# The beginning of an encoder block in written order: x loaded first, projection blocks two rows at a time

## The chip, the cores and the metric

The kernel runs on one core of one Trainium2 chip. The metric is device time in microseconds (us) of one execution. A core has engines that each work through a queue of their own: TensorE (PE, matmuls; loads of its stationary operand are shown apart as PEld), VectorE (DVE), ScalarE (ACT), GpSimd (POOL) and SyncE (SP), which here issues most of the transfers. [...]

## The reference

One layer of a streaming encoder block on 512 tokens of 1024 features, in float32. What matters here is its beginning:

```python
c_act = jax.nn.silu(c)
ada = c_act @ w_ada[l] + b_ada[l]
sh1, sc1, g1, sh2, sc2, g2 = jnp.split(ada, 6, axis=-1)
h = modulate(rmsnorm(x, norm1_g[l]), sh1, sc1)
z = h @ w_in[l]
gate_b, gate_c, xa, xr, gr = jnp.split(
    z, [CONV_W, 2 * CONV_W, 3 * CONV_W, 3 * CONV_W + LRU_W], axis=-1)
```

Then follow a gated convolution and a gated recurrence on the parts of `z` (the mixer), an output projection with a residual, a second norm, and a retrieval over 16384 experts: queries, top-16 searches, and two large products with the expert tables.

## The kernel before

Features lie on the 128 partitions, tokens along the free axis, so x is eight "rows" of 128 x 512 (`xs`). float32 products are made of three matmuls each: a weight and an activation are split into a high and a low part, and `mm3` (L87) adds high x high, high x low and low x high for each of the eight rows. A projection block is 128 columns of `w_in`: 24 matmuls of 128x128 on 128x512 into one PSUM tile `ps_z`, of which there are three. `load_w` loads a block (512 KB), `split_w` makes its high part on ACT (L75) and its low part on DVE (L80). There are 20 blocks; their order is `order` (L120).

The beginning does this, in program order:

- L49 to L63: small parameters, the identity matrix, constants. `ii`, the integers from which the identity is made, lies in a pool that is closed at once, and `xs` may use its place.
- L95: x in four transfers.
- L194: `cs`, the silu of c. L228: squares of the eight rows on ACT, added up on DVE (L217); column sums by matmul (L200); the root, `rstd1`; spread over all partitions by eight matmuls (`rows_of`, L225) into `psr`.
- L272: four times a "quarter" (`ada_quarter`): it clears a PSUM tile on DVE (L240), loads four pieces of the adaLN weights and multiplies them with `cs` (L245), copies the result (ACT, L248), transposes it (L251), and makes shift and scale of two rows (L256 to L258). Then these two rows are multiplied with `psr` (L275) and modulated (L266 to L268: DVE, ACT, DVE), which gives the high and low part of `h`. A block of `w_in` is loaded between.
- L283 to L311: some 35 tiny operations on 128x4 values for the recurrence's decay.
- L319: a constant matrix of means; L325: `ada_rest`, a generator whose steps make the later adaLN sums (gates and second norm) in between the projection blocks: on TensorE (L139) and on DVE (L156, L160), both from `cs`. Its first step clears `bdr` and loads the recurrence's weights into it.
- L391: the mixer: five projection blocks in each of four rounds (`zblock`), each used by ACT and DVE as soon as it is there.

The order on each engine is not the written one here: up to the two large products a planner arranges all instructions, by the program's order, by what waits for what, and by costs it assumes. Only from L1124 on does the kernel use `tc.manual_schedule()`, a region in which each engine issues its instructions as they are written. Instructions from outside such a region may still be put in between.

Of the kernel before, what the change touches and what calls it, by code (L numbers as in the profile page):

```python
# [34 lines left out]
def block_kernel(ctx, tc, xT, small, w_ada1, w_ada, b_ada, w_in, w_r, w_i, w_out, w_q, keys, uT, u, v, final_g, out):  # L35
# [15 lines left out]
    boot = ExitStack()  # L51
    ii = boot.enter_context(tc.tile_pool(name="boot", bufs=1)).tile([128, 128], I32, name="ii")
# [100 lines left out]

    def ada_sum(q, every):
        acc = piece(0, q, "wacc", 2)
        nc.vector.tensor_scalar(acc, acc, cs[:, 0:1], None, op0=OP.mult)  # L156
        for k in range(1, KB):
            if k % every == 0:
                yield
            nc.vector.scalar_tensor_tensor(acc, piece(k, q), cs[:, k:k + 1], acc, op0=OP.mult, op1=OP.add)  # L160
        return acc

    def ada_gate1():
        pr = ada_rows()
# [58 lines left out]
    def rows_of(ps, rstd):  # L223
        for t in range(NT):
            nc.tensor.matmul(ps[:, t * 128:(t + 1) * 128], rstd[:, t:t + 1].to_broadcast([128, 128]), ident,  # L225
                             start=True, stop=True)

    for k in range(KB):  # L228
        sq_sum(k, False)
    rstd1 = const.tile([128, NT], F32, name="rstd1")  # L230
    rsqrt_small(rstd1, pst, 1.0 / D, NT)
    psr = psA.tile([128, T], F32, name="ps_rs")
    rows_of(psr, rstd1)
# [4 lines left out]
    def ada_quarter(j):  # L238
        pr = psZ.tile([128, 256], F32, name="ps_g", bufs=2)
        nc.vector.memset(pr, 0.0)  # L240
        for k2 in range(4):
            wt = ada0.tile([128, 2, 2, 256], F32, name="wada0")
            nc.sync.dma_start(wt.rearrange("p a b c -> p (a b c)"), w_ada1[4 * j + k2])
            for b in range(4):
                nc.tensor.matmul(pr[32 * b:32 * b + 1, :], cs[:, 2 * k2 + b // 2:2 * k2 + b // 2 + 1],  # L245
                                 wt[:, b // 2, b % 2, :], start=(k2 == 0), stop=(k2 == 3), skip_group_check=True)
        row = ada0.tile([128, 256], F32, name="row0", bufs=2)
        nc.scalar.activation(row, pr, AF.Copy)  # L248
        pc = psA.tile([128, 2, 128], F32, name="ps_row")
        for i in range(2):  # L250
            nc.tensor.transpose(pc[:, i, :], row[:, i * 128:(i + 1) * 128], ident)  # L251
# [6 lines left out]
        nc.vector.scalar_tensor_tensor(A1[:, ks], adac[:, 8 + 2 * j:10 + 2 * j], 1.0, sm("n1g")[:, ks],  # L258
                                       op0=OP.add, op1=OP.mult)

    A1 = const.tile([128, KB], F32, name="A1")
    h1h, h1l = h2h, h2l

# [8 lines left out]
    for j in range(4):  # L272
        ada_quarter(j)
        for k in (2 * j, 2 * j + 1):
            nc.vector.tensor_mul(xn1[:, k, :], xs[:, k, :], psr)  # L275
# [7 lines left out]
    sp = const.tile([128, 4], F32, name="sp")  # L283
    l4 = const.tile([128, 8, 4], F32, name="l4")
    lam = sm("lam")
    z_, tn, e_, w_, w2, ac = (l4[:, i, :] for i in range(6))
    nc.vector.tensor_scalar(z_, lam, -1.0, None, op0=OP.mult)
    nc.vector.tensor_tensor(z_, z_, lam, op=OP.max)
    nc.scalar.activation(tn, z_, AF.Tanh, scale=1.0 / 16)
    nc.vector.tensor_scalar(e_, tn, 1.0, None, op0=OP.add)  # L290
    nc.vector.reciprocal(e_, e_)
    nc.vector.tensor_scalar(tn, tn, -1.0, 1.0, op0=OP.mult, op1=OP.add)
    nc.vector.tensor_mul(e_, e_, tn)
    for _ in range(3):
        nc.vector.tensor_mul(e_, e_, e_)
    nc.vector.tensor_scalar(w_, e_, 2.0, None, op0=OP.add)
    nc.vector.reciprocal(w_, w_)
    nc.vector.tensor_mul(w_, w_, e_)
    nc.vector.tensor_mul(w2, w_, w_)
    nc.vector.memset(ac, 1.0 / 15)  # L300
    for n in range(6, -1, -1):
        nc.vector.tensor_mul(ac, ac, w2)
        nc.vector.tensor_scalar(ac, ac, 1.0 / (2 * n + 1), None, op0=OP.add)
    nc.vector.tensor_mul(ac, ac, w_)
    nc.vector.tensor_scalar(z_, lam, -1.0, 0.0, op0=OP.mult, op1=OP.max)
    nc.vector.tensor_scalar(ac, ac, 8.0, None, op0=OP.mult)
    nc.vector.scalar_tensor_tensor(sp, z_, 4.0, ac, op0=OP.mult, op1=OP.add)
    rg = const.tile([128, 4, 4], F32, name="rg")
    sph, spn, brh, bih = (rg[:, i, :] for i in range(4))
    for dst, src, f in ((sph, sp, 0.5), (spn, sp, -1.0), (brh, sm("br"), 0.5), (bih, sm("bi"), 0.5)):  # L310
        nc.vector.tensor_scalar(dst, src, f, None, op0=OP.mult)  # L311
# [7 lines left out]
    hmean = pers2.tile([128, 128], FR, name="sqa")  # L319
    nc.vector.memset(hmean.bitcast(F32), 0.0)  # L320
    for s in range(2):
        nc.vector.tensor_scalar(hmean[64 * s:64 * s + 64, 64 * s:64 * s + 64], iota[64 * s:64 * s + 64, 0:64],
                                0.0, 1.0 / 64, op0=OP.mult, op1=OP.add)
# [1047 lines left out]
```

## Time and profile before

| | |
|---|---|
| median of 3 runs | 1340.93 us (1340.7 to 1341.18) |
| profiled execution | 1340.21 us |
| its span | 1338.4 us |
| first transfer of x issued | 7.41 us |
| first projection matmul (L89) | 26.87 us |
| first output block evicted (L396) | 46.80 us |
| output projection begins on PE | 164.10 us |

The span is what the profile covers of the execution: from the first to the last instruction. A line of the timeline gives start, duration, engine, line, operation, what it writes and reads, shapes, a count, and in brackets how long its engine had been idle before and whom it waited for. A line of a view by stretches gives the stretch, its length, then busy time and number of instructions of each engine, then TensorE's granted clock (1.00 is full), the share of time in which the DMA engines worked, and GB/s. A step of the chain of waits gives start, duration and what.

### The profile page before, as it was taken

How to read it: one execution, taken by the hardware profiler on the slowest of the kernel's cores; microseconds unless marked ns; L12 is line 12 of the kernel's file. 1: busy time of each engine (PE TensorE's matmuls, PEld its weight loads, DVE VectorE, ACT ScalarE, POOL GpSimd, SP SyncE). 2: the span in 40 equal slices, each digit the busy share in tenths (PEclk: the TensorE clock that was granted, in tenths of full speed). 3: DMA queues.
4: the chain of work that ended last, by engine and by line, in shares of the span. 5: the costliest groups of instructions: out<-in, count | busy, mean ns of one | idle time of the engine just before them, and what ended most of it. 6: DMA issues, size and time to landing. Idle time of an engine off the chain costs nothing.

```text
span 1338.4 us, 21113 instructions
## 1 busy us (share of the span) xinstructions
PE 1300.5 (97%) x7408; PEld 1116.9 (83%) x7408; DVE 1218.1 (91%) x2259; ACT 728.1 (54%) x1319; POOL 506.5 (38%) x336
## 2 busy tenths in 40 slices
PE   5999998999899999999999999999999999999996
PEld 2678776777899999999999998888888888888885
DVE  6899876889999999999989869899989899999898
ACT  4667735423576988878759743333433434333333
POOL 0000000000234113455555627577656565645640
PEclk9999998999999999999999999999999999999999
DMA  9684544242798989999999999999999999999993
GB/s 363 230 297 157 170 146 87 72 167 97 271 352 303 337 314 355 400 396 404 417 395 417 416 370 392 374 396 415 414 414 413 415 413 416 412 410 411 415 373 137
DMA packets 150266, 440.03 MB, mean 329 GB/s; under 512 B 16016, under 2 KB 43664, under 8 KB 150160
## 3 DMA queue, kind: packets, MB, share of 16 engines
q1 hardware_dynamic: 103008, 267.23, 53.6%
q0 software_dynamic: 46864, 170.41, 32.5%
q8 instruction: 58, 0.95, 0.3%
q10 hardware_dynamic: 288, 1.05, 0.2%
q14 instruction: 48, 0.39, 0.1%
HBM read 393.54 MB, written 45.09 MB: 328 GB/s over the span
## 4 chain that ended last, share of the span: by engine, by line
PE 65%; DVE 20%; DMA 6%; issue 5%; ACT 3%; POOL 1%; SPq 0%; DVEq 0%; ACTq 0%; POOLq 0%
PE acc L1196 33%; PE ps_z L89 5%; PE ps_z L90 4%; DVE wlo L80 4%; PE ps_z L91 4%; PE ps_act L89 4%; PE ps_act L91 4%; PE ps_act L90 4%; DVE scr L917 3%; DVE oh L728 2%; DMA wraw<-in_uT_dram 2%; PE ps_gt L761 1%; DMA raw<-in_v_dram 1%; DVE rep L543 1%; ACT igh L749 1%
## 5 line engine op out<-in xcount | busy, mean ns | idle before, releaser
L75 ACT ACTIVATE whi<-wraw 128x1024 fp32r<-128x1024 f32 x255 | 269.9, 1059 | 244.1 <-DMA wraw<-in_v_dram 102.0
L80 DVE TENSOR_TENSOR wlo<-wraw,whi 128x1024 fp32r<-128x1024 f32 x255 | 311.0, 1220 | 45.1 <-ACT whi L75 44.5
L89 PE MATMUL ps_act<-h,whi 128*128 128x320 f32 x928 | 291.4, 314 | 0.0
L91 PE MATMUL ps_act<-h,wlo 128*128 128x320 f32 x928 | 287.0, 309 | 0.9 <-issue 0.9
L90 PE MATMUL ps_act<-h,whi 128*128 128x320 f32 x928 | 286.8, 309 | 0.0
L896 POOL DMA_INDIRECT rows<-in_u_dram,idx_s x128 | 207.5, 1621 | 140.3 <-DVE scr L917 111.7
L896 POOL DMA_INDIRECT rows<-in_v_dram,idx_s x128 | 200.7, 1568 | 152.2 <-DVE ys L934 132.0
L1196 PE MATMUL acc<-whi,cl 128*128 128x512 f32 x744 | 229.1, 389 | 0.1
L1196 PE MATMUL acc<-wlo,ch 128*128 128x512 f32 x744 | 229.1, 389 | 0.0
L1196 PE MATMUL acc<-whi,ch 128*128 128x512 f32 x744 | 229.1, 389 | 0.0
L896 POOL DMA_INDIRECT rows<-in_u_dram,idx_b x64 | 92.0, 1438 | 220.3 <-DVE scr L917 157.5
L91 PEld LDWEIGHTS ps_act<-h,wlo 128*128 128x128 f32 x928 | 174.2, 188 | 1.3 <-issue 1.1
L89 PEld LDWEIGHTS ps_act<-h,whi 128*128 128x128 f32 x928 | 174.2, 188 | 1.1
L90 PEld LDWEIGHTS ps_act<-h,whi 128*128 128x128 f32 x928 | 174.4, 188 | 0.2
L934 DVE SCALAR_TENSOR_TENSOR ys<-rows,acts,ys 128x1024 f32<-128x1024 f32 x127 | 163.3, 1286 | 1.4
L1196 PEld LDWEIGHTS acc<-whi,cl 128*128 128x128 f32 x744 | 139.6, 188 | 29.5 <-DVE cl L1087 0.5
L1196 PEld LDWEIGHTS acc<-wlo,ch 128*128 128x128 f32 x744 | 139.7, 188 | 29.1
L1196 PEld LDWEIGHTS acc<-whi,ch 128*128 128x128 f32 x744 | 139.5, 188 | 28.5
L917 DVE SCALAR_TENSOR_TENSOR scr<-rows,h2n 128x1024 f16<-128x1024 f32 x128 | 156.3, 1221 | 5.9 <-DMA rows<-in_u_dram,idx_s 4.3
L1001 ACT ACTIVATE act<-ps_act 128x320 f32<-128x320 f32 x127 | 56.0, 441 | 101.9 <-PE ps_act L91 64.7
L749 ACT ACTIVATE igh<-oh,gl 128x128 f16<-128x128 f16 x320 | 99.6, 434 | 4.1 <-DVE oh L728 4.1
L488 POOL DMA_DIRECT2D x1d<-xn x8 | 4.6, 570 | 252.2 <-ACT xn L487 251.7
(309 smaller groups left out, 1926.6 us busy)
## 6 DMA issues: line engine op xcount, KB each, us to landing
wraw<-in_uT_dram SPq DMA_DIRECT2D x120, 512.0 KB
wraw<-in_v_dram SPq DMA_DIRECT2D x103, 512.0 KB
Gd<-stg SPq DMA_DIRECT2D x46, 512.0 KB
wada<-in_w_ada_dram SPq DMA_DIRECT2D x45, 512.0 KB
Ad<-act SPq DMA_DIRECT2D x48, 320.0 KB
act<-Ad SPq DMA_DIRECT2D x48, 320.0 KB
raw<-in_v_dram SPq DMA_DIRECT2D x25, 512.0 KB
h<-Gd SPq DMA_DIRECT2D x12, 1024.0 KB
```

The lines of the kernel that those rows point to most:

```text
L75: nc.scalar.activation(hi, raw, AF.Copy)
L80: nc.vector.tensor_sub(lo, raw, hi.bitcast(F32))
L89: nc.tensor.matmul(ps, hi[:, k, :], xh(k), start=first and k == ks[0], stop=False)
L90: nc.tensor.matmul(ps, hi[:, k, :], xl(k), start=False, stop=False)
L91: nc.tensor.matmul(ps, lo[:, k, :], xh(k), start=False, stop=last and k == ks[-1])
L728: nc.vector.tensor_tensor(flat.rearrange("p (q n b) -> p q n b", q=8, b=2), io2[:, None, :, :].to_broadcast(shp), sij[:, a0].rearrange("p ...
L749: nc.scalar.activation(ig[:, 1, k // 2, :, k % 2], of[:, k // 2, 0, :, k % 2], AF.Copy, scale=gl[:, t0 + k:t0 + k + 1])
L896: nc.gpsimd.indirect_dma_start(out=r[:, :], out_offset=None, in_=table, in_offset=bass.IndirectOffsetOnAxis(ap=idxs[:, k:k + 1], axis=0))
L917: nc.vector.scalar_tensor_tensor(scr, rows.pop(n), 1.0, hn, op0=OP.mult, op1=OP.mult, accum_out=dst[:, k:k + 1])
L934: nc.vector.scalar_tensor_tensor(ys, rows.pop(k), acts[:, k:k + 1], ys, op0=OP.mult, op1=OP.add)
L1001: nc.scalar.activation(act[c // 2][:, c % 2], ps, AF.Gelu)
L1196: nc.tensor.matmul(accs[b][e], st[:, bs], mv[:, e * 512:(e + 1) * 512], start=first, stop=last)
```

## The change

The whole beginning, from the first load to the first three projection blocks, is put into a `manual_schedule` region, and is written out in an order by hand.

- `ii` takes a place in the ring of low weight parts; x is loaded right behind the small parameters.
- The decay operations become a generator, `decay`, of which a few are made at a time.
- 30 matmuls of the identity with itself are written ahead of the column sums.
- The root is made by `Abs_reciprocal_sqrt` and four DVE operations instead of `Sqrt`, a reciprocal and five more.
- All loads of blocks and quarters are issued in turn (`quarter_load`); `ada_quarter` is cut into `quarter_mm` (one piece) and `quarter_cols`; `zrows(i, j)` does the six matmuls of block i on the rows 2j and 2j+1. For the first three blocks these are put between the quarters' steps; `zblock` then only hands them out.
- Later adaLN sums read `cl`, a copy of `cs` that is written near the region's end.
- The clearing of `bdr` and the matrix of means move into the region.

```diff
+    begin = ExitStack()
+    begin.enter_context(tc.manual_schedule())
...
-            nc.vector.scalar_tensor_tensor(acc, piece(k, q), cs[:, k:k + 1], acc, op0=OP.mult, op1=OP.add)
+            nc.vector.scalar_tensor_tensor(acc, piece(k, q), cl[:, k:k + 1], acc, op0=OP.mult, op1=OP.add)
...
+    decay_it = decay()
+    next(decay_it)
+    warm = psZ.tile([128, T], F32, name="ps_z", bufs=3)
+    for i in range(NW):
+        nc.tensor.matmul(warm[:, i % 4 * 128:(i % 4 + 1) * 128], ident, ident, start=True, stop=True)
     for k in range(KB):
         sq_sum(k, False)
+        next(decay_it, None)
...
+    def quarter_load(j):
         for k2 in range(4):
...
+    def quarter_mm(j, k2):
+        if k2 == 0:
+            pieces[j] = psZ.tile([128, 256], F32, name="ps_g", bufs=2)
+            nc.vector.memset(pieces[j], 0.0)
+        pr, wt = pieces[j], pieces.pop((j, k2))
+        for b in range(4):
+            nc.tensor.matmul(pr[32 * b:32 * b + 1, :], cs[:, 2 * k2 + b // 2:2 * k2 + b // 2 + 1],
+                             wt[:, b // 2, b % 2, :], start=(k2 == 0), stop=(k2 == 3), skip_group_check=True)
+        if k2 == 3:
+            row = ada0.tile([128, 256], F32, name="row0", bufs=2)
+            nc.scalar.activation(row, pr, AF.Copy)
+            pieces[j] = row
...
+    def zrows(i, j):
+        n = order[i]
+        if n not in zps:
+            zps[n] = psZ.tile([128, T], F32, name="ps_z", bufs=3)
+        for k in (2 * j, 2 * j + 1):
+            mm3(zps[n], *zsp[n], hx, lx, [k], k == 0, k == KB - 1)
+
+    def xn_rows(j):
+        for k in (2 * j, 2 * j + 1):
+            nc.vector.tensor_mul(xn1[:, k, :], xs[:, k, :], psr)
...
+    def scaled(j):
+        quarter_cols(j)
         for k in (2 * j, 2 * j + 1):
             modulate(xn1[:, k, :], k, A1, adac[:, 0:8], h1h, h1l)
+
+    for j in range(4):
         if j < 3:
             raws[order[j]] = load_w(w_in[order[j]])
+        quarter_load(j)
+    split(0)
+    quarter_mm(0, 0)
+    quarter_mm(0, 1)
+    rows_of(psr, rstd1)
+    xn_rows(0)
+    quarter_mm(0, 2)
+    quarter_mm(0, 3)
+    for _ in range(6):
+        next(decay_it, None)
+    scaled(0)
+    split(1)
+    xn_rows(1)
+    quarter_mm(1, 0)
+    quarter_mm(1, 1)
+    zrows(0, 0)
+    quarter_mm(1, 2)
+    quarter_mm(1, 3)
+    zrows(1, 0)
...
+    scaled(1)
+    split(2)
+    xn_rows(2)
+    quarter_mm(2, 0)
+    quarter_mm(2, 1)
+    zrows(0, 1)
+    quarter_mm(2, 2)
+    quarter_mm(2, 3)
+    zrows(1, 1)
+    for _ in decay_it:
+        pass
+    scaled(2)
+    xn_rows(3)
+    zrows(2, 0)
+    quarter_mm(3, 0)
+    quarter_mm(3, 1)
+    quarter_mm(3, 2)
+    quarter_mm(3, 3)
+    zrows(2, 1)
+    scaled(3)
+    bdr = wring.tile([128, KB, 128], F32, name="wraw", bufs=WR)
+    nc.vector.memset(bdr, 0.0)
+    nc.vector.tensor_copy(cl, cs)
+    for j in (2, 3):
+        for i in range(3):
+            zrows(i, j)
+    begin.close()
     a0.close()
```

More of the change, by code (lines that the diff above doesn't have):

```diff
@@ L46, in sm @@
         return small_sb[:, o + lo:o + lo + (w if n is None else n)]
+    begin = ExitStack()
+    begin.enter_context(tc.manual_schedule())
     small_sb = const.tile([128, NSMALL], F32, name="small_sb")
     nc.sync.dma_start(small_sb, small)
-    boot = ExitStack()
-    ii = boot.enter_context(tc.tile_pool(name="boot", bufs=1)).tile([128, 128], I32, name="ii")
+    ii = wring.tile([128, KB, 128], I32, name="wlo", bufs=WB)[:, 0, :]
     nc.gpsimd.iota(ii, pattern=[[1, 128]], base=0, channel_multiplier=-1)
@@ L155, in ada_sum @@
         acc = piece(0, q, "wacc", 2)
-        nc.vector.tensor_scalar(acc, acc, cs[:, 0:1], None, op0=OP.mult)
+        nc.vector.tensor_scalar(acc, acc, cl[:, 0:1], None, op0=OP.mult)
         for k in range(1, KB):
@@ L194, in block_kernel @@
     cs = const.tile([128, KB], F32, name="cs")
+    cl = const.tile([128, KB], F32, name="cl8")
     nc.scalar.activation(cs, sm("c"), AF.Silu)
@@ L226, in rows_of, with decay @@
                              start=True, stop=True)
+    sp = const.tile([128, 4], F32, name="sp")
+    l4 = const.tile([128, 8, 4], F32, name="l4")
+    rg = const.tile([128, 4, 4], F32, name="rg")
+    sph, spn, brh, bih = (rg[:, i, :] for i in range(4))
+    def decay():
+        lam = sm("lam")
+        z_, tn, e_, w_, w2, ac = (l4[:, i, :] for i in range(6))
+        nc.vector.tensor_scalar(z_, lam, -1.0, None, op0=OP.mult)
+        nc.vector.tensor_tensor(z_, z_, lam, op=OP.max)
+        nc.scalar.activation(tn, z_, AF.Tanh, scale=1.0 / 16)
+        nc.vector.tensor_scalar(e_, tn, 1.0, None, op0=OP.add)
+        nc.vector.reciprocal(e_, e_)
+        nc.vector.tensor_scalar(tn, tn, -1.0, 1.0, op0=OP.mult, op1=OP.add)
+        nc.vector.tensor_mul(e_, e_, tn)
+        for _ in range(3):
+            yield
+            nc.vector.tensor_mul(e_, e_, e_)
+        yield
+        nc.vector.tensor_scalar(w_, e_, 2.0, None, op0=OP.add)
+        yield
+        nc.vector.reciprocal(w_, w_)
+        yield
+        nc.vector.tensor_mul(w_, w_, e_)
+        yield
+        nc.vector.tensor_mul(w2, w_, w_)
+        nc.vector.memset(ac, 1.0 / 15)
+        for n in range(6, -1, -1):
+            yield
+            nc.vector.tensor_mul(ac, ac, w2)
+            yield
+            nc.vector.tensor_scalar(ac, ac, 1.0 / (2 * n + 1), None, op0=OP.add)
+        yield
+        nc.vector.tensor_mul(ac, ac, w_)
+        nc.vector.tensor_scalar(z_, lam, -1.0, 0.0, op0=OP.mult, op1=OP.max)
+        yield
+        nc.vector.tensor_scalar(ac, ac, 8.0, None, op0=OP.mult)
+        yield
+        nc.vector.scalar_tensor_tensor(sp, z_, 4.0, ac, op0=OP.mult, op1=OP.add)
+        for dst, src, f in ((sph, sp, 0.5), (spn, sp, -1.0), (brh, sm("br"), 0.5), (bih, sm("bi"), 0.5)):
+            nc.vector.tensor_scalar(dst, src, f, None, op0=OP.mult)
@@ L228, in block_kernel @@
+    decay_it = decay()
[3 more added lines that the diff above has]
+        nc.tensor.matmul(warm[:, i % 4 * 128:(i % 4 + 1) * 128], ident, ident, start=True, stop=True)
     for k in range(KB):
         sq_sum(k, False)
+        next(decay_it, None)
     rstd1 = const.tile([128, NT], F32, name="rstd1")
-    rsqrt_small(rstd1, pst, 1.0 / D, NT)
+    mean1, half1 = (const.tile([128, 64], F32, name=n)[:, :NT] for n in ("rs_m", "rs_t"))
+    nc.vector.tensor_scalar(mean1, pst, 1.0 / D, EPS, op0=OP.mult, op1=OP.add)
@@ L232, in block_kernel @@
+    nc.scalar.activation(rstd1, mean1, AF.Abs_reciprocal_sqrt)
+    nc.vector.tensor_mul(half1, rstd1, rstd1)
+    nc.vector.scalar_tensor_tensor(half1, half1, -0.5, mean1, op0=OP.mult, op1=OP.mult)
+    nc.vector.scalar_tensor_tensor(rstd1, half1, 1.5, rstd1, op0=OP.add, op1=OP.mult)
     psr = psA.tile([128, T], F32, name="ps_rs")
-    rows_of(psr, rstd1)
     a0 = ExitStack()
@@ L236, in block_kernel, with quarter_cols @@
     xn1 = ada0.tile([128, KB, T], F32, name="xn1", bufs=1)
-    def ada_quarter(j):
-        pr = psZ.tile([128, 256], F32, name="ps_g", bufs=2)
-        nc.vector.memset(pr, 0.0)
+    pieces, zps = {}, {}
+    def quarter_load(j):
         for k2 in range(4):
[L242 to L248, printed above, removed]
+            pieces[j, k2] = ada0.tile([128, 2, 2, 256], F32, name="wada0")
+            nc.sync.dma_start(pieces[j, k2].rearrange("p a b c -> p (a b c)"), w_ada1[4 * j + k2])
+    def quarter_mm(j, k2):
[10 more added lines that the diff above has]
+            pieces[j] = row
+    def quarter_cols(j):
+        row = pieces.pop(j)
         pc = psA.tile([128, 2, 128], F32, name="ps_row")
@@ L259, in ada_quarter, with split @@
                                        op0=OP.add, op1=OP.mult)
+    hx = lambda k: h1h[:, k, :]
+    lx = lambda k: h1l[:, k, :]
+    def zrows(i, j):
[7 more added lines that the diff above has]
+            nc.vector.tensor_mul(xn1[:, k, :], xs[:, k, :], psr)
+    def split(j):
+        zsp[order[j]] = split_w(raws[order[j]])
     A1 = const.tile([128, KB], F32, name="A1")
@@ L270, in modulate @@
             full(k, f)
[L272 to L275, printed above, removed]
+    def scaled(j):
+        quarter_cols(j)
         for k in (2 * j, 2 * j + 1):
             modulate(xn1[:, k, :], k, A1, adac[:, 0:8], h1h, h1l)
+    for j in range(4):
         if j < 3:
             raws[order[j]] = load_w(w_in[order[j]])
-    a0.close()
-    sp = const.tile([128, 4], F32, name="sp")
-    l4 = const.tile([128, 8, 4], F32, name="l4")
@@ L285, in block_kernel @@
[L285 to L311, printed above, removed]
+        quarter_load(j)
[5 more added lines that the diff above has]
+    quarter_mm(0, 2)
@@ new lines, in block_kernel @@
+    quarter_mm(0, 3)
[10 more added lines that the diff above has]
+    zrows(1, 0)
+    hmean = pers2.tile([128, 128], FR, name="sqa")
+    nc.vector.memset(hmean.bitcast(F32), 0.0)
+    for s in range(2):
+        nc.vector.tensor_scalar(hmean[64 * s:64 * s + 64, 64 * s:64 * s + 64], iota[64 * s:64 * s + 64, 0:64],
+                                0.0, 1.0 / 64, op0=OP.mult, op1=OP.add)
@@ new lines, in block_kernel @@
+    for _ in range(6):
+        next(decay_it, None)
+    scaled(1)
[20 more added lines that the diff above has]
+    nc.vector.memset(bdr, 0.0)
@@ L318, in block_kernel @@
     bdl = mixp.tile([128, KB, 128], FR, name="bdl")
[L319 to L323, printed above, removed]
     def ada_rest():
-        bdr = wring.tile([128, KB, 128], F32, name="wraw", bufs=WR)
-        nc.vector.memset(bdr, 0.0)
         for s in range(2):
@@ L347, in block_kernel @@
     mix = mx.enter_context(tc.tile_pool(name="mix", bufs=1))
-    hx = lambda k: h1h[:, k, :]
-    lx = lambda k: h1l[:, k, :]
     def zblock(n, name):
@@ L358, in zblock @@
                 zsp[order[j]] = split_w(raws[order[j]])
+        if n in zps:
+            next(ada_it, None)
+            return zps.pop(n)
         hi, lo = zsp[n]
@@ L1323 @@
 VT = 4
+NW = 30
 def arrays(I):
```

4 lines of the change are left out of this document (1 added, 3 removed).

## The prediction

> **What bounds the kernel now.** I read the page first: the busy shares and the chain that ended last.
>
> ```profile
> PE 1300.5 (97%) x7408; PEld 1116.9 (83%) x7408; DVE 1218.1 (91%) x2259; ACT 728.1 (54%) x1319; POOL 506.5 (38%) x336
> ...
> PE 65%; DVE 20%; DMA 6%; issue 5%; ACT 3%; POOL 1%; SPq 0%; DVEq 0%; ACTq 0%; POOLq 0%
> ```
>
> These are averages over the whole kernel; the change touches only the beginning. So I read the stretches from 41 us on (first column of this view: PE busy, then PEld, DVE, ACT, POOL).
>
> ```profile
> 41.00:53.90 12.90, 12.90 (x61) 8.30 (x54) 11.13 (x21) 9.66 (x13) 0.00 (x0) 1.00 0.95 354
> 60.00:160.00 100.00, 99.95 (x451) 77.14 (x450) 93.45 (x128) 72.60 (x101) 0.00 (x0) 1.00 0.61 207
> 160.00:210.00 50.00, 49.16 (x210) 38.38 (x209) 36.29 (x43) 20.63 (x28) 0.00 (x0) 1.00 0.46 143
> ```
>
> TensorE has no hole from 41 to 210 us but 0.9 us (0.05 + 0.84): the projections and the output projection stand on it back to back. Whatever moves the time at which TensorE has its first three blocks behind it moves the end by about as much, since nothing of those 169 us can be packed tighter. The measure of the beginning is therefore this: when are the 72 matmuls of the first three blocks done? The view of `ps_z` by stretches, and some steps of the chain (start, us, what; 0.23 us per matmul), give it:
>
> ```profile
> 0.00:40.00 40.00, 7.72 (x24) 4.04 (x25) 0.00 (x0) 0.00 (x0) 1.00 0.79 309
> 40.00:50.00 10.00, 8.15 (x32) 5.23 (x30) 0.00 (x0) 2.24 (x4) 1.00 0.99 359
> 50.00:53.90 3.90, 3.50 (x15) 2.92 (x16) 0.00 (x0) 0.00 (x0) 1.00 0.86 294
> ```
>
> ```profile
> 47.89 0.96 PE ps_row L139 x4
> 48.85 0.43 PE ps_z L90
> ...
> 49.51 0.96 PE ps_row L139 x4
> 50.47 0.43 PE ps_z L89
> ...
> 53.19 0.23 PE ps_z L91
> ```
>
> 24 + 32 + 15 = 71, so the 72nd ends at about 53.9. By then TensorE has also done two groups of the later sums (L139): 0.96 us each, and the matmul behind each takes 0.43 instead of 0.23: 2 x 1.16 = 2.3. The change keeps those behind, so the fair mark is 53.9 - 2.3 = **51.6 us**.
>
> **The change, part by part.** First what it gains. x is loaded first instead of behind the first quarter of adaLN weights and one block.
>
> ```profile
> 1.20 1.84 SPq L243 DMA_DIRECT2D wada<-in_w_ada_dram  x4
> ...
> 4.89 0.16 DVE L298 TENSOR_TENSOR l<-l 128x4 f32<-128x4 f32 x1
> 5.09 0.16 DVE L299 TENSOR_TENSOR l<-l 128x4 f32<-128x4 f32 x1
> ...
> 5.43 2.17 PE L245 MATMUL ps_g<-wada,cs 128*1 128x256 f32 x16 [5.43 <-DMA wada<-in_w_ada_dram]
> ...
> 9.19 1.03 PE L245 MATMUL ps_g<-wada,cs 128*1 128x256 f32 x8 [0.19 <-DMA wada<-in_w_ada_dram]
> ...
> 12.34 1.30 ACT L215 ACTIVATE sq<-xs 128x512 f32<-128x512 f32 x2
> ...
> 13.08 5.46 DVE L217 TENSOR_TENSOR sqa<-sqa,sq 128x512 f32<-128x512 f32 x7
> ...
> 18.69 1.84 PE L200 MATMUL ps_col<-ones,sqa 128*128 128x1 f32 x8 [0.81 <-DVE sqa L217]
> ...
> 22.21 0.16 DVE L118 TENSOR_TENSOR rstd<-rstd,rs_t 128x4 f32<-128x4 f32 x1
> ...
> 23.12 2.01 PE L225 MATMUL ps_rs<-ident,rstd 128*128 128x128 f32 x8
> ...
> 25.16 1.29 DVE L275 TENSOR_TENSOR xn<-xs,ps_rs 128x512 f32<-128x512 f32 x2 [2.80 <-PE ps_rs L225]
> ```
>
> The four x pieces, of the same 512 KB, land where the first four weight pieces land now: 5.4 to 9.2. Two squares (1.30) and seven adds (5.46) end at about 12.3 instead of 18.5; the column sums (1.84) at 14.2; the root, in four small DVE steps and one ACT step (0.2 each, and hand-overs), at 15.4 instead of 22.4. The thirty warm-up matmuls lie in the wait for x and cost nothing (0.25 us each by the L225 row, 7.5, from 1.6 on; the cover is 12.3). The small decay steps, 0.2 us each by the rows of 4.89 and 5.09, hide between the adds or in later waits; without cover the twenty steps left would cost 4 us.
>
> From here the written order of each engine decides, and this is the core of my forecast. In the new code the clearing of a quarter's PSUM row (L240) is issued on DVE by the first call of `quarter_mm`, that is, **behind** `split` and `xn_rows`. Before, it was free to run early:
>
> ```profile
> 0.93 0.55 DVE L240 MEMSET ps_g<- 128x256 f32 x2
> ...
> 10.80 0.27 DVE L240 MEMSET ps_g<- 128x256 f32 x1 [1.81 <-ACT row L248]
> ...
> 33.34 0.27 DVE L240 MEMSET ps_g<- 128x256 f32 x1
> ```
>
> Now queued behind it: on TensorE, which writes that row, the quarter's sixteen matmuls, and in written order behind these the `zrows` steps, the transposes of `scaled`, and so again DVE. For quarter 0 the low half (1.1, waiting for its high half on ACT, to 16.9) and the clearing come first, to 17.2; then two pieces (2.06 at the cold rate of the 9.19 row), then `rows_of` (2.01): 21.4. The row of 25.16 above is thus only some 3.7 us earlier, though the root is 7.0 earlier.
>
> Then each quarter is a ring: DVE, TensorE, DVE. Its terms:
>
> ```profile
> 25.05 0.61 PE L245 MATMUL ps_g<-wada,cs 128*1 128x256 f32 x8
> ...
> 26.17 0.44 PE L251 MATMUL ps_row<-ident,row 128*128 128x128 f32 x2 [0.50 <-ACT row L248]
> ...
> 30.00 1.52 ACT L267 ACTIVATE h<-xn,adac,A 128x512 fp32r<-128x512 f32 x2 [1.53 <-DVE A L258]
> ...
> 31.40 1.28 DVE L268 TENSOR_TENSOR h<-mfull,h 128x512 fp32r<-128x512 f32 x2
> ...
> 36.39 1.22 DVE L80 TENSOR_TENSOR wlo<-wraw,whi 128x1024 fp32r<-128x1024 f32 x1
> ...
> 44.30 1.29 DVE L268 TENSOR_TENSOR h<-mfull,h 128x512 fp32r<-128x512 f32 x2
> ```
>
> DVE: low half 1.2, two rows of `xn` 1.2, clearing 0.3: 2.7. TensorE: four pieces at 0.61 and twelve matmuls at 0.23, 5.2; transposes 0.44. DVE: three small steps 0.6, and the modulation of two rows, 30.00 to 32.68, 2.65. With 0.1 or so of hand-over, 11.7 us for quarters 1 and 2. Quarter 3 has no low half and only one `zrows` between: 9.2. The splits, `xn`, decay and mean-matrix steps lie in the ring or beside TensorE's part. The weights aren't late: 5 pieces per quarter at 1.26 us (by the 5.43 and 9.19 rows' spacing) are 6.3, and the last lands at about 33.
>
> With TensorE at full clock the last modulation ends at 26.4 + 11.7 + 11.7 + 9.2 = 59.0 (now 44.30 + 1.29 = 45.6), and the 36 matmuls of the last two row pairs end at about 63.6: **12.0 us later** than 51.6.
>
> That is the lower end. The other end is the clock. In each ring TensorE stands still while DVE works: 0.6 + 2.65 + 2.7 = 5.9 us. What a pause does shows where the kernel now pauses on the way to the queries:
>
> ```profile
> 215.70 1.77 PE L225 MATMUL ps_rs<-ident,rstd 128*128 128x128 f32 x8 [0.94 <-DVE rstd L118]
> ...
> 219.09 0.80 PE L89 MATMUL ps_z<-h,whi 128*128 128x512 f32 x1 [1.62 <-ACT h L267]
> ...
> 222.98 0.40 PE L91 MATMUL ps_z<-h,wlo 128*128 128x512 f32 x1
> ```
>
> ```profile
> 216.00:222.00 6.00, 4.38 (x21) 2.69 (x19) 4.50 (x9) 2.61 (x4) 0.22 (x1) 0.51 0.76 12
> ```
>
> After pauses of 0.94 and 1.62 us the granted clock is 0.51 for six microseconds, and from the return to work at 219.09 to the first quick matmul at 222.98 pass 3.9 us. With 3.9 us of each ring at about 1.7 to 1.9 times the time (1.03 against 0.61 above), a ring is some 1.9 us longer, the start 0.8: 27.2 + 13.5 + 13.6 + 10.8 = 65.1, and the 72nd matmul at 69.8: **18.2 us later**. Pauses of 5.9 us are longer than those that cut the clock in the row, so I take this end, and 12.0 as the bound.
>
> [...]
>
> What can come back: the 0.9 us of hole between 60 and 210, and in the pauses DVE and ACT may split blocks 3 to 5 ahead. The latter buys nothing while TensorE is the limit; it costs nothing if DVE's lag of some 4 us (the mixer's first input is at T - 2.8 instead of T - 7) dissolves in DVE's 6.5 us of slack between 60 and 160. 18.2 less 0.9 is 17 us. The profiled execution took 1340.2 us (span 1338.4): 1340.2 + 17 = **1357**; the median of the three runs, 1340.93, lies 0.7 above it, inside the rounding.
>
> **The rivals.**
> 1. *The written order with the clock whole*: 12.0 less 0.9, 1351 to 1353. For it: TensorE works 5 of every 11.7 us. Against: the 0.51 row. It lies on my side.
> 2. *Not slower: the clearing doesn't stand in the ring.* If the four clearings sit ahead of `split` and `xn` on DVE, quarter matmuls run under the modulation, a ring falls to about 7.5 us (DVE's own work), the last modulation ends at 43.4 to 44.2 and the 72nd matmul at 48.1 to 48.9: 2.7 to 3.5 faster, 1337. It decides at one place: whether L240's four steps come before or after the two `xn` rows of their quarter. Against it: the region orders every engine as written, and the clearing is inside `quarter_mm`.
> 3. *The delay is lost later*: DVE-limited stretches between 60 and 160 swallow it, 1340 to 1343. Against it: 99.95 of 100 us busy on TensorE.
> 4. *The region doesn't bind the order*, so that the planner undoes it: then only x first is left, within 3 us of now.
>
> **How the numbers follow.** Forecast with the clock cut 0.58; rival 1 0.2; rival 2 0.14; rivals 3 and 4 together 0.08. The likeliest case alone is 1353 to 1362: the clock's 3.9 us may be 3 to 6 (67 to 73), and the planner's order of the later prologue may shift by 3. The range for 8 in 10 reaches down through rival 1 to the lower edge of rival 3: 1340 to 1363, and leaves out rival 2 and the tails. A measurement of this kernel can tell about 0.2%, 2.7 us, from no change. Slower takes the forecast and rival 1, 0.78; rival 2 lies at the bound: 0.1 of it faster, and the rest, 0.12 with rivals 3 and 4, same.
>
> **What would show it.** Right: L240's rows directly behind the two L275 rows of their quarter and the quarter's first L245 waiting for DVE; holes of 5 to 6 us on TensorE between about 22 and 65 with a granted clock near 0.5; last L268 of the beginning near 65, and from about 70 on TensorE dense as before. Wrong: L245 of quarter 1 during the first modulation (rival 2), the clock at 1.00 throughout (rival 1), or holes on TensorE after 75 us, which would mean that another engine has become the limit. If the last piece of weights lands well after 33 us, loads of the later sums were let in between.

## The result and the profile after

The changed kernel takes 1360.05 us (median of 4 runs, 1358.87 to 1361.12), the kernel before, measured beside it, 1341.06 us (1340.7 to 1343.3). The ratio is 1.0143, with a 95% interval of 1.0128 to 1.0158: 19 us slower. The profiled execution took 1361.12 us, its span is 1359.4 us; that is 20.9 us over the profiled execution before.

The first two lines to compare are the busy times and the chain of work that ended last, from the page of the changed kernel:

```profile
PE 1310.8 (96%) x7468; PEld 1128.8 (83%) x7468; DVE 1219.8 (90%) x2258; ACT 728.3 (54%) x1319; POOL 503.4 (37%) x336
...
PE 70%; DVE 14%; DMA 9%; issue 4%; ACT 2%; DVEq 0%; SPq 0%; ACTq 0%
```

TensorE still has 96% of busy time (10 us of it are the new warm-ups); where 19 us are lost can't be seen in such an average. The view by stretches of the changed kernel shows it (columns as before: stretch, length, PE, PEld, DVE, ACT, POOL, granted clock, DMA share, GB/s):

```profile
10.00:15.00 5.00, 2.28 (x19) 2.00 (x18) 3.15 (x12) 3.37 (x5) 0.00 (x0) 0.92 1.03 420
15.00:20.00 5.00, 3.80 (x24) 2.21 (x24) 1.05 (x2) 0.00 (x0) 0.00 (x0) 0.50 1.04 424
...
25.00:30.00 5.00, 1.36 (x16) 0.40 (x16) 4.59 (x13) 0.60 (x1) 0.00 (x0) 0.50 1.03 418
30.00:35.00 5.00, 5.00 (x31) 2.27 (x23) 0.37 (x3) 0.00 (x0) 0.00 (x0) 0.53 1.03 420
...
45.00:50.00 5.00, 5.00 (x27) 2.83 (x28) 0.00 (x0) 0.39 (x1) 0.00 (x0) 0.66 0.00 0
...
60.00:160.00 100.00, 96.93 (x433) 73.67 (x433) 93.33 (x129) 71.47 (x98) 0.00 (x0) 1.00 0.61 203
160.00:210.00 50.00, 47.70 (x208) 36.11 (x207) 42.04 (x57) 28.08 (x41) 0.00 (x0) 1.00 0.49 153
```

From 25 to 30 us VectorE works (4.59 of 5) and TensorE hardly does (1.36); from 30 to 35 it is the other way round (5.00 and 0.37). The engines take turns, and TensorE takes its turns at a mean clock of 0.50 to 0.66. The last two rows answer to those of before: TensorE, which had 99.95 of 100 us and 49.16 of 50, now has 96.93 and 47.70.

The steps themselves, from the timeline of the changed kernel (VectorE and TensorE rows; start, duration, operation, and in brackets the idle time ahead and who ended it):

```profile
15.83 0.27 DVE L300 MEMSET ps_g<- 128x256 f32 x1
16.20 1.89 PE L303 MATMUL ps_g<-wada,cs 128*1 128x256 f32 x16 [3.07 <-issue]
...
25.23 0.69 DVE L348 TENSOR_TENSOR h<-mfull,h 128x512 fp32r<-128x512 f32 x1
25.84 1.22 DVE L79 TENSOR_TENSOR wlo<-wraw,whi 128x1024 fp32r<-128x1024 f32 x1
26.98 1.28 DVE L336 TENSOR_TENSOR xn<-xs,ps_rs 128x512 f32<-128x512 f32 x2
28.31 0.27 DVE L300 MEMSET ps_g<- 128x256 f32 x1
28.64 1.89 PE L303 MATMUL ps_g<-wada,cs 128*1 128x256 f32 x16 [6.13 <-DVE ps_g L300]
33.31 1.72 PE L303 MATMUL ps_g<-wada,cs 128*1 128x256 f32 x16
36.45 0.38 PE L314 MATMUL ps_row<-ident,row 128*128 128x128 f32 x2
36.86 0.16 DVE L319 TENSOR_TENSOR adac<-ps_row,small_sb 128x4 f32<-128x4 f32 x1 [6.42 <-PE ps_row L314]
...
39.55 0.69 DVE L348 TENSOR_TENSOR h<-mfull,h 128x512 fp32r<-128x512 f32 x1
...
42.95 1.89 PE L303 MATMUL ps_g<-wada,cs 128*1 128x256 f32 x16 [6.13 <-DVE ps_g L300]
...
50.87 0.16 DVE L319 TENSOR_TENSOR adac<-ps_row,small_sb 128x4 f32<-128x4 f32 x1 [6.89 <-PE ps_row L314]
...
53.56 0.69 DVE L348 TENSOR_TENSOR h<-mfull,h 128x512 fp32r<-128x512 f32 x1
...
63.76 0.69 DVE L348 TENSOR_TENSOR h<-mfull,h 128x512 fp32r<-128x512 f32 x1
...
69.03 1.04 PE L138 MATMUL ps_row<-wada,cl 128*1 128x512 f32 x8
...
72.31 0.50 PE L90 MATMUL ps_z<-h,wlo 128*128 128x512 f32 x1 [1.58 <-DVE wlo L79]
...
96.63 0.47 PE L471 MATMUL ps_rs<-mt,sqa 128*128 128x512 f32 x1 [1.19 <-DVE sq L477]
...
182.78 0.50 PE L471 MATMUL ps_rs<-mt,sqa 128*128 128x512 f32 x1 [2.29 <-ACT mt L467]
...
184.97 0.39 PE L88 MATMUL ps_z<-ybuf_h,whi 128*128 128x512 f32 x1
```

One ring is read like this. VectorE ends a modulation (25.23 + 0.69), makes a low half (L79), two rows of `xn` (L336), and only then clears the next quarter's PSUM row (L300, 28.31). TensorE has waited 6.13 us for just that clearing, by its bracket. Then TensorE does the quarter and twelve matmuls of row pairs, and VectorE waits 6.42 us for the transposes. The modulations end at 25.9, 40.2, 54.3 and 64.5: rings of 14.3, 14.0 and 10.2 us. The first group of later sums (69.03) stands directly behind the 72nd projection matmul, so its start is the mark for the end of the beginning: 69.0, against the 51.6 that the prediction set for the kernel before (52.7 is fairer, as is worked out behind the experiments). The output projection starts at 184.97, 20.9 us later than before (164.10). In the profiled executions all of the loss lies ahead of it.

### The profile page after: what moved, and what is told of

It reads as the page before. It is cut to its first block, busy times and chain, and to the rows that moved or that the text cites. A ratio compares the mean times of both kernels' runs of the same rounds, so it can differ in the third digit from the quotient of the medians.

```text
span 1359.4 us, 21242 instructions
## 1 busy us (share of the span) xinstructions
PE 1310.8 (96%) x7468; PEld 1128.8 (83%) x7468; DVE 1219.8 (90%) x2258; ACT 728.3 (54%) x1319; POOL 503.4 (37%) x336
## 3 DMA queue, kind: packets, MB, share of 16 engines
q10 hardware_dynamic: 288, 1.05, 0.2%
## 4 chain that ended last, share of the span: by engine, by line
PE 70%; DVE 14%; DMA 9%; issue 4%; ACT 2%; DVEq 0%; SPq 0%; ACTq 0%
PE acc L1294 25%; PE ps_act L88 9%; PE ps_act L89 9%; PE ps_act L90 9%; DMA wraw<-in_v_dram 5%; PE ps_z L88 4%; PE ps_z L89 4%; PE ps_z L90 4%; PE ps_gt L859 3%; DVE scr L1015 2%; DVE wlo L79 2%; DMA raw<-in_v_dram 1%; PE ps_g L303 1%; DMA x1d<-xn 1%; DVE rep L641 1%
## 5 line engine op out<-in xcount | busy, mean ns | idle before, releaser
L79 DVE TENSOR_TENSOR wlo<-wraw,whi 128x1024 fp32r<-128x1024 f32 x255 | 311.0, 1220 | 40.1 <-ACT whi L74 39.5
L1294 PEld LDWEIGHTS acc<-whi,ch 128*128 128x128 f32 x744 | 139.5, 188 | 28.6
```

The costliest lines, as they stand in the source:

```text
L79: nc.vector.tensor_sub(lo, raw, hi.bitcast(F32))
L1294: nc.tensor.matmul(accs[b][e], st[:, bs], mv[:, e * 512:(e + 1) * 512], start=first, stop=last)
```

## The experiments

Two numbers are followed in all of them: the start of the first later sums (69.03 above), and the sum of TensorE's holes from there to the output projection (5.4 us in the changed kernel, summed over 10 us stretches; the three large ones are the last three brackets above). The theory is that of the prediction: the clearing stands in the ring, the pauses cut the clock, and everything behind TensorE's first three blocks follows by as much.

**Clearings issued early.**

```diff
+    def quarter_clear(j):
+        pieces[j] = psZ.tile([128, 256], F32, name="ps_g", bufs=2)
+        nc.vector.memset(pieces[j], 0.0)
...
+    quarter_clear(0)
+    quarter_clear(1)
     split(0)
...
     scaled(0)
+    quarter_clear(2)
...
     scaled(1)
+    quarter_clear(3)
```

> The changed kernel with nothing but the four clearings of a quarter's PSUM row issued earlier on VectorE: quarters 0 and 1 ahead of the first low half, quarter 2 behind the first modulation, quarter 3 behind the second. Theory (the clearing closes a ring VectorE, TensorE, VectorE): the quarter's first matmuls run under the modulation, quarter 0 begins at about 13.1 us instead of 16.2, and a ring is 0.6 + 2.65 + 1.2 on VectorE, 1.4 + 0.5 + 0.44 on TensorE and ScalarE, 7 to 8.5 us instead of 14; last modulation of the beginning at 42 to 48 us instead of 64.4, the 72nd projection matmul at 47 to 53 instead of 68.9, time 1337 to 1345. Rival (the pauses and the cut clock, or the weights, set the ring whatever the clearing does): rings stay over 11 us, time over 1352.

Measured: 1341.49 us, ratio to the kernel before 1.0003 (0.9990 to 1.0016). From the timeline of this kernel:

```profile
24.60 0.27 DVE L299 MEMSET ps_g<- 128x256 f32 x1
...
25.26 1.04 PE L304 MATMUL ps_g<-wada,cs 128*1 128x256 f32 x16
...
30.36 0.49 PE L88 MATMUL ps_z<-h,whi 128*128 128x512 f32 x1 [1.28 <-ACT h L348]
...
43.75 0.69 DVE L349 TENSOR_TENSOR h<-mfull,h 128x512 fp32r<-128x512 f32 x1
...
49.01 1.04 PE L138 MATMUL ps_row<-wada,cl 128*1 128x512 f32 x8
```

Four instructions of 0.27 us, moved by a few lines, are worth 18.6 us. The 6.13 us pauses are gone; the longest left in a ring is 1.28. The rings are 7.8, 7.0 and 5.2 us instead of 14.3, 14.0 and 10.2; the last modulation ends at 44.4 instead of 64.5, and the later sums start at 49.0 instead of 69.0. The clearing in the ring was the cause. (Quarter 0 began at 14.96 us and not at 13.1 as expected: its clearing, at 14.59, still stands behind the root's steps on VectorE.) What the mark wins against the kernel before (3.7 us, from 52.7) is given back in holes: 4.4 us until the output projection, against 0.9 before.

**Extra matmuls in the pauses**, with the clearing left where it is. They compute nothing that is used. First 18 for each ring:

```diff
+        if j < 3:
+            spin = psA.tile([128, T], F32, name="ps_col")
+            for i in range(NB):
+                nc.tensor.matmul(spin[:, i % 4 * 128:(i % 4 + 1) * 128], ident, ident, start=True, stop=True)
```

> The changed kernel with extra matmuls of the identity that compute nothing that is used: 8 behind the column sums, 18 behind the transposes of each of the first three quarters, so that TensorE works through its pauses while the clearing stays where it is. Theory (pauses of 6 us cut the granted clock, and the cut clock makes TensorE's part of each ring longer): granted clock near 1.00 between 15 and 60 us, rings of 11.7 to 12.3 us instead of 14.3 and 14.0, 72nd projection matmul at 63 to 64.5 instead of 68.9, time 1353 to 1356. Rival (the clock is not what makes the ring long; hand-overs and waits are): no change within 1 us, or slower by up to 2 where the extra matmuls overrun the pause.

Measured: 1355.18 us (ratio 1.0096, 1.0067 to 1.0126). The time is the theory's, but by luck, for the steps to it are not: the rings were 13.0 and 13.1 us, the mark 66.3, and the clock still fell (0.66 and 0.80 in the stretches from 30 and from 45 us). The holes behind the mark had shrunk to 3.8 us, which was not forecast. Pauses of 2.47 and 2.11 us remained. So the same with 28 for each ring, 40 warm-ups and 10 behind the column sums:

> The kernel with extra matmuls in TensorE's pauses, with enough of them that no pause of 2 us is left: 40 instead of 30 warm-ups, 10 behind the column sums, 28 behind the transposes of each of the first three quarters. Theory (what was left of the cut clock with 18 came from the pauses of 2.5 and 2.1 us that stayed): granted clock 0.9 or more throughout from 15 to 60 us, rings of 11.7 to 12.2 instead of 13.0 and 13.1, the third 9.2, 72nd projection matmul at 62.5 to 64.5 instead of 66.2, time 1351 to 1353.5. Rival (the clock is cut for another reason than the pauses): rings stay at 13, time 1354 to 1357.

Measured: 1353.10 us (1.0095, 1.0075 to 1.0114). Timeline and view by stretches of this kernel:

```profile
24.47 0.69 DVE L350 TENSOR_TENSOR h<-mfull,h 128x512 fp32r<-128x512 f32 x1
...
27.87 1.04 PE L305 MATMUL ps_g<-wada,cs 128*1 128x256 f32 x16 [0.23 <-DVE ps_g L302]
30.43 1.04 PE L305 MATMUL ps_g<-wada,cs 128*1 128x256 f32 x16
...
36.02 0.69 DVE L350 TENSOR_TENSOR h<-mfull,h 128x512 fp32r<-128x512 f32 x1
...
47.62 0.69 DVE L350 TENSOR_TENSOR h<-mfull,h 128x512 fp32r<-128x512 f32 x1
...
64.31 1.04 PE L138 MATMUL ps_row<-wada,cl 128*1 128x512 f32 x8
```

```profile
25.00:30.00 5.00, 4.77 (x45) 3.74 (x44) 4.30 (x14) 0.00 (x0) 0.00 (x0) 1.00 1.03 417
30.00:35.00 5.00, 5.00 (x44) 3.65 (x43) 1.26 (x5) 1.47 (x3) 0.00 (x0) 1.00 1.02 415
```

With the clock at 1.00 the rings are 11.55 and 11.6 us, and half a quarter takes 1.04 us instead of 1.89. So of a ring of 14.3 us, the cut clock makes 2.7; of the 11.6 that are left, the clearing's place makes some 4, since the early clearings alone gave 7.8 and 7.0. The third ring (11.4, expected 9.2) was not shortened: there the 28 extra matmuls overran a pause of only 3.6 us. Together the extra work gains 7 us of 19.

**Block 3 split inside the region.**

```diff
         quarter_load(j)
+    raws[order[3]] = load_w(w_in[order[3]])
...
     scaled(3)
+    split(3)
```

> The changed kernel with block 3 loaded behind the last quarter's weights and split inside the written region, behind the last modulation. Theory (the 1.58 us hole of TensorE at 72.3 is block 3's late low half, one of three holes that the sum left out): that hole goes and the end with it, time 1 to 2 us less than the changed kernel, 1358 to 1359, unless the first output block's chain on VectorE and ScalarE is pushed back by the 1.2 us of the split and opens a wider hole later (96.6 or 182.8), which would leave the time as it is. Rival (VectorE and ScalarE are behind altogether after 65 us, and any hole closed opens elsewhere): no change, 1359.5 to 1361.

Measured: 1354.42 us (1.0098, 1.0077 to 1.0119). The mark is the same as in the changed kernel, but from the timeline of this kernel:

```profile
68.97 1.04 PE L138 MATMUL ps_row<-wada,cl 128*1 128x512 f32 x8
...
93.38 0.50 PE L473 MATMUL ps_rs<-mt,sqa 128*128 128x512 f32 x1 [0.28 <-ACT mt L469]
...
178.28 0.50 PE L473 MATMUL ps_rs<-mt,sqa 128*128 128x512 f32 x1 [1.47 <-ACT mt L469]
...
181.36 0.39 PE L88 MATMUL ps_z<-ybuf_h,whi 128*128 128x512 f32 x1
```

I had expected 1 to 2 us, and it gained 5.6. The holes went from 5.4 to 1.8, and the output projection starts 3.6 us earlier: one late split of 1.2 us had drawn the later holes behind it as well. The other 2 us lie behind the output projection, where a second pause on the way to the queries is gone. In the changed kernel it is this row; the kernel before has one of 1.19 at the same place, and the early clearings alone leave one of 2.10:

```profile
247.43 0.73 PE L88 MATMUL ps_z<-h,whi 128*128 128x512 f32 x2 [2.08 <-ACT h L347]
```

It is gone in every kernel below that splits block 3 in the region. Why (the planner's order changes behind it) was not tried.

**The same code in the planner's order**: the region taken away, and no warm-ups.

```diff
-    begin.enter_context(tc.manual_schedule())
...
-NW = 30
+NW = 0
```

> The changed kernel without its region of written order, and without the thirty warm-up matmuls (the planner would put them behind the identity, which it makes late): the same loads, pieces, decay and row pairs, in the planner's order. Theory (it is the written order, not x first or two rows at a time, that costs the 20 us): the clearings go ahead, no ring is left, x is there 4 us earlier; 72nd projection matmul at 46 to 52, time 1335 to 1343. Rival (splitting the first blocks by row pairs, or the changed order of the loads, costs as much whatever the order): over 1350.

Measured: 1345.94 us (1.0037, 1.0023 to 1.0051). So 14 us of the 19 come from the written order and not from what it orders. But it is slower than I expected, and slower than before. The 72nd matmul ends at 55.9 in this kernel, not at 46 to 52.

**x first and nothing else**, in the kernel before.

```diff
-    boot = ExitStack()
-    ii = boot.enter_context(tc.tile_pool(name="boot", bufs=1)).tile([128, 128], I32, name="ii")
+    ii = wring.tile([128, KB, 128], I32, name="wlo", bufs=WB)[:, 0, :]
...
-    boot.close()
```

> The kernel before with x loaded first and nothing else: the integers for the identity take a place in the ring of low weight parts, so that x need not wait for them. Theory (x first moves the root by some 6 us, but the weights of all four quarters move 5 us back, and TensorE, which begins its projection rows between 26 and 44 us, is limited by VectorE's and TensorE's work more than by x): 72nd projection matmul, without later sums, 1 to 4 us earlier than 51.6, time 1337 to 1340. Rival (the later weights become what is late): 72nd matmul after 52, time 1341 to 1346.

Measured: 1343.44 us (1.0029, 1.0017 to 1.0042). The rival's time held, but not its reason: no weights were late (from the column sums to the 72nd matmul none of TensorE's waits is for a load). From VectorE's timeline of this kernel:

```profile
22.22 1.28 DVE L266 TENSOR_TENSOR h<-mfull,h 128x512 fp32r<-128x512 f32 x2
...
37.28 0.16 DVE L254 TENSOR_TENSOR adac<-ps_row,small_sb 128x4 f32<-128x4 f32 x1 [5.15 <-PE ps_row L249]
...
46.55 0.16 DVE L254 TENSOR_TENSOR adac<-ps_row,small_sb 128x4 f32<-128x4 f32 x1 [5.35 <-PE ps_row L249]
...
48.38 1.29 DVE L266 TENSOR_TENSOR h<-mfull,h 128x512 fp32r<-128x512 f32 x2
```

The first modulation ends at 23.5 us instead of 28.6, but the last one at 49.7 instead of 45.6. Before quarters 2 and 3 VectorE waits 5.15 and 5.35 us for the transposes, while TensorE, 5.00 of 5 us busy from 30 to 35, does projection rows that the early x has set free. The planner, too, built the ring: TensorE's row pairs ahead of the matmuls that VectorE needs. The kernel in the planner's order above has the same two waits, 5.06 and 4.54 us. This is read from the rows; no run changed the place of the row pairs in the planner's order. The clock had a part in it as well: from 25 to 30 us it was 0.74 with x first, and 1.00 in the kernel before.

**Both mended.** Clearings early and block 3 split in the region:

> The changed kernel with both edits that were tried one at a time: the four clearings issued earlier, and block 3 loaded behind the last quarter's weights and split inside the region behind the last modulation. Theory (time follows two numbers: the end of the 72nd projection matmul, and the sum of TensorE's holes from there to the output projection, 4.4 us with the early clearing alone): 72nd matmul at 49 us as with the early clearing alone, the 1.6 us hole on block 3's low half gone and the holes after it smaller, in all 1 to 3 us; 1336 to 1340, at or just under the kernel before. Rival (VectorE and ScalarE are behind, so that the same holes open in other places): 1341 to 1342, no change against the early clearing alone.

Measured: 1333.11 us, ratio 0.9947 (0.9933 to 0.9962): 0.5% faster than the kernel before, and 3 us better than expected. From its timeline:

```profile
49.10 1.04 PE L138 MATMUL ps_row<-wada,cl 128*1 128x512 f32 x8
...
158.59 0.50 PE L478 MATMUL ps_rs<-mt,sqa 128*128 128x512 f32 x1 [0.28 <-ACT mt L474]
159.62 0.39 PE L88 MATMUL ps_z<-ybuf_h,whi 128*128 128x512 f32 x1
```

The two edits act on different terms: the early clearing on the mark (49.1), the split on the holes (0.4 us). The output projection starts 4.5 us earlier than in the kernel before; the rest of the gain lies behind it, where the second pause is gone (1.19 before), and is explained only in part.

**More reordering on top of both.** In one kernel: all sixteen matmuls of the next quarter ahead of the row pairs, splits one step later, decay at the end.

```diff
+    for k2 in range(4):
+        quarter_mm(1, k2)
+    quarter_clear(2)
+    xn_rows(1)
+    zrows(0, 0)
```

> The changed kernel with the written order mended: clearings early, all sixteen matmuls of the next quarter directly behind a quarter's transposes and ahead of the row pairs that need the modulation, low halves of blocks 1 and 2 one step later, most of the decay and the matrix of means behind the last modulation, block 3 split in the region, the recurrence's weights cleared on GpSimd, 36 warm-ups and 6 extra matmuls behind the column sums. Theory (with the ring open, VectorE's own work sets the beginning: two modulated rows 2.65, three small steps 0.6, two rows of xn 1.2, a low half 1.2, 5.7 us a quarter instead of 7.75): last modulation at 41 to 43 us, 72nd projection matmul at 46 to 48.5, time 1333 to 1338. Rival (TensorE, dense from 35 us with the early clearing, is already the limit, or the delayed decay steps hold up the mixer's first block): 72nd matmul at 49 or later, or holes of over 4 us behind it, time 1339 to 1343.

Measured: 1337.17 us (0.9982, 0.9968 to 0.9996), 4 us worse than without. The later sums start at 52.2. Two rows of its timeline tell why:

```profile
20.46 0.61 PE L306 MATMUL ps_g<-wada,cs 128*1 128x256 f32 x8 [1.78 <-DMA wada<-in_w_ada_dram]
...
31.22 0.50 PE L88 MATMUL ps_z<-h,whi 128*128 128x512 f32 x1 [1.51 <-ACT whi L74]
```

With x loaded first, quarter 1's weights land while TensorE already stands in front of them, and the later split makes TensorE wait for block 1's high half. In this written order both waits, of 1.78 and 1.51 us, held up what was queued behind them. The last modulation ended at 46.3 us, not at 41 to 43; that the time still lies in the theory's range is luck. What the two waits make and what the clock makes (0.68 and 0.71 in the stretches from 20 and 30 us, where the kernel with both edits had 0.99 and 1.00) was not taken apart.

Then, on the kernel with both edits, 40 warm-ups and 10 extra matmuls behind the column sums:

> The kernel with early clearings and block 3 split in the region, and TensorE kept busy up to quarter 0: 40 warm-ups instead of 30 and 10 extra matmuls behind the column sums. Theory (there the granted clock was 0.82 and 0.50 from 10 to 20 us, after pauses of 1.4 us ahead of and behind the column sums; at full clock quarter 0's two halves and the spreading of the root take 1.04, 1.16 and 1.04 us instead of 1.89, 2.08 and 1.79): first modulation ends 2 us earlier, 72nd projection matmul at 47 to 48 instead of 49, time 1331 to 1332.5. Rival (the weights of the next quarters land too late for it, or VectorE's rings take it up): 72nd matmul at 49, 1333 to 1334, no change.

Measured: 1336.37 us (0.9965, 0.9954 to 0.9976). That is 2 us and more above what theory and rival had. The clock was 1.00 from 10 to 30 us, but the first modulation ended only half a microsecond earlier, not 2: the 40 warm-ups ran until 13.2 us, and the column sums began at 13.04 instead of 12.15. The later sums started at 49.6: nothing gained at the mark, as the rival said. A wait of 1.7 us for weights at 58.8 and one of 2.24 at 163.0 made most of the 4.1 us of holes, in a profiled execution (1339.01 us) that was the slowest of eleven. And last, the same with the recurrence's tile cleared on GpSimd:

```diff
-    nc.vector.memset(bdr, 0.0)
+    nc.gpsimd.memset(bdr, 0.0)
```

> The same, with the recurrence's weight tile cleared on GpSimd instead of VectorE, so that the loads that wait for it on SyncE's queue, and the loads of blocks 4 and 5 behind them, aren't held up by VectorE's place in the written order. Theory (that queue stood idle between 33 and 65 us in the changed kernel for this): loads of blocks 4 and 5 issued 3 us or more earlier, time up to 1 us less. Rival (TensorE has no hole there any more that a load could close): no change within 1 us.

Measured: 1333.28 us (0.9944, 0.9927 to 0.9961), 3 us under the one ahead of it, where at most 1 was expected (the two intervals overlap a little): the recurrence's loads leave SyncE's queue at 26.9 us instead of 47.3, a block's load behind them at 37.4 instead of 50.1, and the holes are 0.5 us. It is level with the kernel that has the two edits alone; the extra matmuls brought nothing. Nor was the clock whole: from 30 to 35 us both warm kernels had 0.66, where the two edits alone had 1.00.

The kernels with the written region in one table, in us (mark: start of the first later sums; holes: TensorE's, from the mark to the output projection):

| kernel | mark | holes | output projection | median | ratio to before |
|---|---|---|---|---|---|
| changed | 69.0 | 5.4 | 185.0 | 1360.05 | 1.0143 |
| block 3 split | 69.0 | 1.8 | 181.4 | 1354.42 | 1.0098 |
| 18 extra matmuls | 66.3 | 3.8 | 180.6 | 1355.18 | 1.0096 |
| 28 extra matmuls | 64.3 | 2.4 | 176.8 | 1353.10 | 1.0095 |
| reordered | 52.2 | 0.8 | 163.7 | 1337.17 | 0.9982 |
| clearings early | 49.0 | 4.4 | 164.1 | 1341.49 | 1.0003 |
| both, warm | 49.6 | 4.1 | 164.2 | 1336.37 | 0.9965 |
| both, warm, GpSimd | 49.3 | 0.5 | 159.9 | 1333.28 | 0.9944 |
| both | 49.1 | 0.4 | 159.6 | 1333.11 | 0.9947 |

In every row the output projection less mark and holes is 110.0 to 110.7 us. That is TensorE's own work between the two, the same in all of them. (So it is in the kernel before, if its mark is set at 52.7: 164.1 less 52.7 and 0.9 is 110.5.) (With the early clearings alone, two matmuls of the output projection go ahead of the last hole, at 162.8; the third is counted.) Behind the output projection there is a scatter: the median less the output projection's start is 1172 to 1177 us (1176.8 for the kernel before). So mark and holes don't give the order of the lower rows: with the reordered kernel and the early clearings the output projection starts within 0.5 us, and the times are 4 us apart.

## Why the prediction was right, and the step that was off

- **The ring.** It was forecast that L300 stands directly behind the two `xn` rows and that the quarter waits for VectorE; the 6.13 us brackets say so, and moving the clearing alone takes 18.6 us away. The fourth rival, a region that doesn't bind the order, is out by the same rows. A ring at full clock was worked out as 11.7 us from seven rows of the old profile; with the clock kept up it was 11.55 and 11.6.
- **x first.** Squares and sums were put at 12.3 and the root at 15.4; the column sums started at 12.08, and behind the warm-ups they were 1.05 us long instead of 1.84 (1.87 in the two kernels without warm-ups). The thirty warm-ups took 9.8 us, not 7.5, and still ended ahead of the sums, at 11.2; forty did not. The first modulation ended at 25.9 (forecast 27.2: 26.4, for which no sum is shown, and 0.8 for the clock), since the clearing came at 15.83 and not at 17.
- **The clock.** It was cut (0.50 and 0.53 in the stretches from 25 to 35 us), as the row at 216 us had it (0.51). The ring's surcharge was set at 1.9 us and measured at 2.7 and 2.4: TensorE, back at 28.64 after a pause of 6.13, had its first quick matmul at 35.3, 6.7 us later and not 3.9. The third ring, with a shorter pause, came to 10.2 (forecast 10.8). The errors cancel by luck: the 72nd matmul was forecast at 69.8, and the later sums behind it start at 69.0.
- **The clock ahead of quarter 0.** The pause there was 3.07 us, and the stretch from 15 to 20 us had 0.50, so the 0.8 us stood rightly in the sum. The stretch from 10 to 15 us has 0.92: in the changed kernel the granted clock was 1.00 from 14.0 to 14.2 us, 0.60 from 14.2 to 14.4 and 0.50 from 14.4 to 15.0. So the cut began at about 14.2, when the pause (from 13.13) was 1.1 us old.
- **What comes back: the mis-sized term.** This is the step that failed. The prediction took 0.9 us of holes as recouped and said that VectorE's lag dissolves in its slack. Instead the holes grew to 5.4: the term was mis-sized by 5.4 us (4.5 more holes in place of 0.9 fewer). It had named holes after 75 us as a sign of being wrong, and two of the three large ones are that (1.19 at 96.6, 2.29 at 182.8). The third rival, that later stretches swallow the delay, is out: they added to it. Block 3 was not split ahead in the pauses, though its load was issued at 32.67 us, no load was under way from 45 to 50 (the row of that stretch), and VectorE stood idle for 6.89 us up to 50.87: the planner put the split behind the first output block, at 71.04, and TensorE, at 72.31, waited for it. Busy VectorE time from 60 to 160 (93.33 of 100) looked like slack in the average, but the mixer's first steps come in a burst: from 61 to 75 us VectorE's rows show one pause, of 0.16. With block 3 split in time, 3.6 us of the holes went.
- **The mark of before.** 51.6 is about 1.1 us too early. It takes 2.3 us off for two groups of the later sums, of four matmuls each. In the changed kernel the same eight are one group (the row of 69.03), which costs 1.2 once: from the last matmul ahead of it, at 68.71, to the second behind it, at 70.34, pass 1.63 us, and 0.46 where no group lies between. 53.9 less 1.2 is 52.7. So the mark moved by 16.3 and not by 17.4, and with 4.5 of holes that is 20.8, against the 20.9 by which the output projection moved. The forecast of 17 came near the 19 of the medians because a mark set too early made up for a part of the holes.
- **The rivals.** The second one, a clearing that isn't in the ring, was priced at 48.1 to 48.9 for the 72nd matmul and 1337; tried, it gave 49.0 and 1341.5, no gain where 2.7 to 3.5 us were forecast, because of the same holes. The first, a whole clock, was 1351 to 1353; tried, 1353.1. That it fits is partly luck: its third ring was 11.4 us and not 9.2, and its holes were 2.4 us and not none. Neither described the changed kernel.

## What to carry to other kernels

When an order is written out by hand, look at what each helper issues on which engine: an instruction of 0.27 us that needs nothing, issued on the first call of a helper, waited here for all that stood ahead of it on its engine (a low half and two rows of `xn`, 2.5 us in the first ring), and closed a ring in which two engines took turns instead of working side by side, three times over. Issue such steps (clearings, copies of constants) as early as their buffer is free, or on an idle engine. And a hand-written stretch must include the first steps of what follows (here the split of the next block and the loads behind it), since the planner that arranges the rest did not put them into the stretch's pauses by itself here; TensorE's holes behind the stretch have to be added up before the gain or loss is believed.

## What the runs showed of the hardware

- **Short pauses cut the clock here, but not always.** Pauses of 2.47 and 2.11 us, in the kernel with 18 extra matmuls, were followed by clocks of 0.66 and 0.80 in the 5 us stretches from 30 and from 45. The same pause of 1.28 us, ahead of the same matmul, left the clock at 1.00 with the early clearing alone and was followed by 0.66 in the warm one. Two rows of the views by stretches, first of the kernel with early clearings, then of the warm one:

```profile
30.00:35.00 5.00, 4.13 (x26) 2.14 (x27) 4.54 (x9) 2.35 (x4) 0.00 (x0) 1.00 1.03 422
```

```profile
30.00:35.00 5.00, 4.78 (x24) 2.12 (x25) 4.78 (x12) 1.74 (x3) 0.00 (x0) 0.66 1.02 418
```

  What made the same pause count in one kernel and not in the other, no run shows.
- **The cut came late once.** After the pause of 2.11 us the first half quarter still took 1.04 us, and the second, 3.5 us later, 1.68. So the matmul behind that pause didn't tell whether the pause was paid for.
- **Extra matmuls held the clock.** 28 of them take 6.42 us; with them, 40 warm-ups and 10 behind the column sums it was 1.00 from 10 to 60 us. But they gained only the cut clock's share of a ring, 2.7 us, and once overran a shorter pause.
